# A batched matrix product: the first batch's x in two whole row tiles and a shared tile with a tail of eight small transfers

## The chip, the cores and the metric

The kernel runs on one core of a Trainium2 chip. The metric is the time of one execution on the device in microseconds (us); less is better. The core has five engines with their own instruction streams: PE (matrix products, with PEld for its weight loads), DVE, ACT, POOL and SP. Sixteen DMA engines move data between the chip's main memory (HBM) and the core's on-chip memory of 128 partitions; SP and POOL issue the transfers here, each on a queue of its own (q1 and q0 in the profile).

## The reference

`out[b] = x[b] @ weight[b]` for 32 batches, all in float32: x is 32 x 512 x 1024, weight is 32 x 1024 x 768, out is 32 x 512 x 768.

```python
def reference(x, weight):
    return np.matmul(x, weight).astype(np.float32)
```

In main memory that is 67.1 MB of x, 100.7 MB of weights and 50.3 MB of results, 218 MB in all, each read or written once.

## The kernel before

For each batch the 512 rows of x are divided into four row tiles of 128. Row `4*i + mt` belongs to tile `mt` and lies in partition `i`, so that a partition's four rows lie side by side in main memory (4 KB a row, 16 KB a partition). PE needs x with its long side (k) on the partitions, so each tile is first transposed on PE against an identity matrix (into PSUM, tile `pt`), and DVE copies the result to `xT` as bfloat16. Then 16 products for each row tile (8 steps of k, two shares of the 768 columns) go into PSUM banks (L123), and ACT and DVE copy the three banks of each pair of row tiles to `out_sb` (L143 to L145).

Weights come by POOL, cast to bfloat16 on the way, in one transfer of 3 MB (as read) for most batches (L70); four buffers. x comes by POOL in pairs of batches, 4 MB as read, also cast (L60); three buffers. Their transposes (L78) take two bfloat16 numbers as one 32-bit word. Results of two batches go out in one transfer by POOL (L164); those of the last four batches go out by SP (L182 to L185 and L216).

The order of the work is written out by hand (`manual_schedule`): each engine executes its instructions in the order of the program. POOL's first issues are w of batch 0, x of batches 1 and 2, w of 1 and 2, x of 3 and 4, w of 3, x of 5 and 6. The sixth and later ones wait for buffers: x of 5 and 6 for that of batch 0's first tiles, w of batch 4 for that of batch 0, which is free when PE has done batch 0, and so on. Batch `b`'s w is issued three batches ahead.

Batch 0 is the exception that the change concerns. Its x comes by SP, uncast, in float32, with transfers that carry no other batch: `x_first` (shown as `x_sb`, in the x pool) holds row tiles 0 to 2, 12 KB a partition, in one transfer (L151); `x_fourth` (shown as `one_sb`, in a pool with one buffer that is used again for the results of batch 30) holds row tile 3, 4 KB a partition, in 17 transfers (L154): 32, 16 and 16 partitions, twice two, and twelve times five, whose partitions are four apart. `transpose_first` takes a tile from one or the other (L101), does eight transposes (L105) and two casts (L106). PE transposes tiles 0 to 2 before its first product; tile 3 is transposed when its products are due:

```python
if b == 0:
    xT = {mt: transpose_first(mt) for mt in range(MT - 1)}
```

The kernel's lines that matter:

Of the kernel before, what the change touches and what calls it, by code (L numbers as in the profile page):

```python
# [8 lines left out]
F32 = mybir.dt.float32  # L9
# [4 lines left out]
def kernel(  # L14
# [6 lines left out]
    nc = tc.nc  # L21
    B, M, K = x.shape
    _, _, N = weight.shape
    P = 128
    MT = M // P
# [10 lines left out]
    x_pool = ctx.enter_context(tc.tile_pool(name="x", bufs=3))  # L36
    xT_pool = ctx.enter_context(tc.tile_pool(name="xT", bufs=6))
    out_pool = ctx.enter_context(tc.tile_pool(name="out", bufs=3))
    one_pool = ctx.enter_context(tc.tile_pool(name="one", bufs=1))
# [7 lines left out]
    x_view = x.rearrange("b (mi mo) k -> b mi mo k", mi=P)  # L47
# [6 lines left out]
    def banks():  # L54
        return [mpsum.tile([P, 512], F32, name=f"pm{i}") for i in range(3)]

    def load_pair(b):

        xs[b] = x_pool.tile([P, 2 * MT, K], BF16, name="x_sb")
        nc.gpsimd.dma_start(out=xs[b], in_=pair_view[b // 2])  # L60

    def load_last():
        xs[B - 1] = x_pool.tile([P, MT, K], BF16, name="x_sb")
        nc.gpsimd.dma_start(out=xs[B - 1], in_=x_view[B - 1])  # L64

    def load_w(b):
        ws[b] = w_pool.tile([P, KT, N], BF16, name="w_sb")
        at = 0
        for n in CHUNKED.get(b, (KT,)):
            nc.gpsimd.dma_start(out=ws[b][:, at:at + n, :], in_=w_view[b, :, at:at + n, :])  # L70
            at += n
# [9 lines left out]
    def transpose_pair(b, mt):  # L81

        both = xT_pool.tile([P, 2, JT, P // 2, 2, 2], BF16, name="xT")
        for half in range(2):
            nc.vector.tensor_copy(  # L85
                both[:, :, :, :, half, :].rearrange("p b j i r -> p j b i r"),
                words(b, mt + MT * half).rearrange("p j (b i r) -> p j b i r", b=2, r=2),
            )
        return [both[:, r].rearrange("p j i h r -> p j (i h) r") for r in range(2)]

    def transpose_last(mt):
        xT = xT_pool.tile([P, JT, P, 2], BF16, name="xT")
        nc.vector.tensor_copy(  # L93
            xT.rearrange("p j m r -> p (j m r)"), words(B - 1, mt).rearrange("p j m -> p (j m)")
        )
        return xT

    def transpose_first(mt):

        xT = xT_pool.tile([P, JT, P, 2], BF16, name="xT")  # L100
        rows = x_first[:, mt] if mt < MT - 1 else x_fourth[:, 0]  # L101
        for h in range(2):
            pt = tpsum.tile([P, JT, P], F32, name="pt")
            for i in range(JT):
                nc.tensor.transpose(pt[:, i, :], rows[:, JT * h + i::KT], ident)  # L105
            nc.vector.tensor_copy(  # L106
                xT[:, 2 * h:2 * h + 2].rearrange("p j m r -> p j r m"),
                pt.rearrange("p (j r) m -> p j r m", r=2),
            )
        return xT  # L110
# [8 lines left out]
    def matmuls(pm, half, xT, b, kos, together):  # L119
        for ko in kos:  # L120
            for i, (bank, at, off, size) in enumerate(SPLITS[half]):
                shares = half == 1 and i == 0
                nc.tensor.matmul(  # L123
                    pm[bank][:, at:at + size],
                    xT[:, ko // 2, :, ko % 2],
                    ws[b][:, ko, off:off + size],
                    start=(ko == 0 and not (together and shares)),
                    stop=(ko == KT - 1),
                    skip_group_check=together,
                )  # L130

    def open_out(b):

        if b == B - 2:
            outs[b] = one_pool.tile([P, MT * N], F32, name="one_sb")
            return
        if b % 2 == 0 or b == B - 1:
            twos[b // 2] = out_pool.tile([P, 2, MT * N], F32, name="out_sb")
        outs[b] = twos[b // 2][:, b % 2]

    def evacuate(b, pair, pm):
        o = outs[b][:, pair * N2:(pair + 1) * N2]
        nc.scalar.copy(o[:, 0:512], pm[0])  # L143
        nc.vector.tensor_copy(o[:, 512:1024], pm[1])  # L144
        nc.scalar.copy(o[:, 1024:N2], pm[2])  # L145

    with tc.manual_schedule():

        x_first = x_pool.tile([P, MT - 1, K], F32, name="x_sb")
        x_fourth = one_pool.tile([P, 1, K], F32, name="one_sb")  # L150
        nc.sync.dma_start(x_first, x_view[0, :, :MT - 1])  # L151
        few = [slice(at, first + 20, 4) for first in (0, 20, 40) for at in range(first, first + 4)]
        for rows in (slice(64, 96), slice(96, 112), slice(112, P), slice(60, 62), slice(62, 64), *few):
            nc.sync.dma_start(x_fourth[rows, 0], x_view[0, rows, MT - 1])  # L154
        load_w(0)
        ident = const.tile([P, P], F32)
        make_identity(nc, ident)
        load_pair(1)
        load_w(1)
        load_w(2)  # L160
        load_pair(3)

        def store(at):
            nc.gpsimd.dma_start(out=two_view[at], in_=twos[at])  # L164

        ready = {}
        for b in range(B):
            if b % 2 and b + AHEAD + 1 < B:
                if b + AHEAD + 1 == B - 1:
                    load_last()  # L170
                else:
                    load_pair(b + AHEAD + 1)
            if b % 2 and 2 < b < B - HELD - AHEAD:
                store((b - 3) // 2)
            if b + AHEAD < B:
                load_w(b + AHEAD)
            if b == B - LATE:
                store(b // 2 - 2)
                store(b // 2 - 1)
            if b == B - 1:  # L180
                halves = [slice(pair * N2, (pair + 1) * N2) for pair in range(2)]
                nc.sync.dma_start(out_view[b - 1, :, halves[0]], outs[b - 1][:, halves[0]])  # L182
                for late in range(B - LATE, B - 2):
                    nc.sync.dma_start(out_view[late], outs[late])
                nc.sync.dma_start(out_view[b - 1, :, halves[1]], outs[b - 1][:, halves[1]])  # L185
            open_out(b)
            if b == 0:
                xT = {mt: transpose_first(mt) for mt in range(MT - 1)}
            elif b == B - 1:
                xT = {mt: transpose_last(mt) for mt in range(MT)}  # L190
            else:
                if b % 2:
                    for mt in range(MT):
                        ready[b, mt], ready[b + 1, mt] = transpose_pair(b, mt)
                xT = {mt: ready.pop((b, mt)) for mt in range(MT)}
            if b not in CHUNKED:
                for pair in range(2):
                    pm = banks()
                    for half in range(2):
                        mt = 2 * pair + half  # L200
                        if mt not in xT:
                            xT[mt] = transpose_first(mt)
                        matmuls(pm, half, xT[mt], b, range(KT), False)
                    evacuate(b, pair, pm)
                continue
            pms = [banks() for _ in range(2)]
            at = 0
            for n in CHUNKED[b]:
                last = at + n == KT
                for mt in range(MT):  # L210
                    matmuls(pms[mt // 2], mt % 2, xT[mt], b, range(at, at + n), True)
                    if last and mt % 2 == 1:
                        pair = mt // 2
                        evacuate(b, pair, pms[pair])
                        if b == B - 1:
                            nc.sync.dma_start(out_view[b, :, halves[pair]], outs[b][:, halves[pair]])  # L216
                at += n
# [30 lines left out]
```

## Time and profile before

| | before |
|---|---|
| median of 3 runs | 514.45 us (514.42 to 514.56) |
| profiled execution | 514.44 us |
| its span, first to last instruction | 512.7 us |
| PE busy (matmuls) | 435.4 us, 85% |
| DVE, ACT, POOL busy | 130.0, 76.1 and 39.1 us |
| main memory, read and written | 167.77 MB and 50.33 MB, 425 GB/s over the span |
| granted TensorE clock, mean | 0.94 |

The profile is that of one execution. The span is what lies between its first and its last instruction; 1.7 us of the execution lie around it. In the rows of engines each digit is the busy share of one of 40 equal slices in tenths. A line of the time order has start, length, engine, line, operation, what it writes and reads, and in brackets how long the engine sat idle before it and what ended that. In the rows of DMA queues stand the packets, the megabytes and the time that their packets took as a share of all sixteen engines. A packet is one run of bytes on one DMA engine; the trace has its start, its length, its size and its queue, but not which of the sixteen engines it was. A transfer ends with a 4-byte packet on each DMA engine that took part: its completion write.

### The profile page before, as it was taken

How to read it: one execution, taken by the hardware profiler on the slowest of the kernel's cores; microseconds unless marked ns; L12 is line 12 of the kernel's file. 1: busy time of each engine (PE TensorE's matmuls, PEld its weight loads, DVE VectorE, ACT ScalarE, POOL GpSimd, SP SyncE). 2: the span in 40 equal slices, each digit the busy share in tenths (PEclk: the TensorE clock that was granted, in tenths of full speed). 3: DMA queues.
4: the chain of work that ended last, by engine and by line, in shares of the span. 5: the costliest groups of instructions: out<-in, count | busy, mean ns of one | idle time of the engine just before them, and what ended most of it. 6: DMA issues, size and time to landing. Idle time of an engine off the chain costs nothing.

```text
span 512.7 us, 5785 instructions
## 1 busy us (share of the span) xinstructions
PE 435.4 (85%) x2576; PEld 278.7 (54%) x2576; DVE 130.0 (25%) x196; ACT 76.1 (15%) x129; POOL 39.1 (8%) x73
## 2 busy tenths in 40 slices
PE   1806999999999996997989989798898989999991
PEld 1504666666666663654646546464464645666660
DVE  0202324141515141320413205041040410514121
ACT  1100121212121201111111111111101111120201
POOL 3000010101010101001010000101001000010000
PEclk9956999999999998997999989899798998999997
DMA  8999999999999999999999999999999999999998
GB/s 240 224 221 213 218 220 216 333 221 310 243 218 336 215 324 231 228 325 220 330 223 234 318 223 334 217 247 304 221 333 218 258 295 220 331 215 212 320 427 345
DMA packets 12712, 135.63 MB, mean 265 GB/s; under 512 B 1296, under 2 KB 1296, under 8 KB 3088
## 3 DMA queue, kind: packets, MB, share of 16 engines
q0 software_dynamic: 11440, 126.88, 96.6%
q1 hardware_dynamic: 1248, 8.39, 4.1%
q8 instruction: 20, 0.33, 0.2%
q14 instruction: 4, 0.03, 0.0%
HBM read 167.77 MB, written 50.33 MB: 425 GB/s over the span
## 4 chain that ended last, share of the span: by engine, by line
PE 46%; DMA 37%; issue 8%; DVE 5%; another core or an unknown queue 1%; POOL 1%; ACT 0%; SPq 0%; POOLq 0%
PE pm L123 40%; DMA w_sb<-in_weight_dram 28%; DMA one_sb<-in_x_dram 8%; PE pt L78 5%; DVE xT L85 4%; DVE out_sb L144 1%; POOL out_dram L164 0%; PE pt L105 0%; POOL w_sb L70 0%; POOL x_sb L60 0%; DVE one_sb L144 0%; DVE xT L93 0%; ACT out_sb L145 0%; SPq L151 0%
## 5 line engine op out<-in xcount | busy, mean ns | idle before, releaser
L123 PE MATMUL pm<-w_sb,xT 128*128 128x256 bf16 (+1 forms) x2048 | 353.7, 336 | 26.4 <-DMA w_sb<-in_weight_dram 26.2
L123 PEld LDWEIGHTS <-xT 128*128 128x128 bf16 x2048 | 205.3, 101 | 170.3 <-DMA w_sb<-in_weight_dram 29.3
L144 DVE COPY out_sb<-pm 128x512 f32<-128x512 f32 x62 | 42.9, 691 | 317.6 <-PE pm L123 317.6
L78 PE MATMUL pt<-ident,x_sb 128*128 128x128 f32 x496 | 79.8, 302 | 10.5 <-DVE xT L85 10.2
L78 PEld LDWEIGHTS pt<-ident,x_sb 128*128 128x128 f32 x496 | 69.3, 209 | 21.5 <-DVE xT L85 18.7
L85 DVE COPY xT<-pt 128x1024 bf16<-128x1024 bf16 x120 | 77.4, 687 | 11.0 <-PE pt L78 11.0
L143 ACT COPY out_sb<-pm 128x512 f32<-128x512 f32 x62 | 36.3, 585 | 271.7 <-PE pm L123 271.7
L145 ACT COPY out_sb<-pm 128x512 f32<-128x512 f32 x62 | 36.3, 585 | 145.7 <-PE pm L123 145.6
L70 POOL DMA_DIRECT2D w_sb<-in_weight_dram x37 | 20.1, 544 | 404.8 <-PE pm L123 397.6
L105 PE MATMUL pt<-ident,one_sb 128*128 128x128 f32 x8 | 1.9, 421 | 19.1 <-DMA one_sb<-in_x_dram 19.1
L106 DVE CAST xT<-pt 128x512 bf16<-128x512 f32 x8 | 5.8, 733 | 34.6 <-PE pt L105 34.1
L105 PE MATMUL pt<-ident,x_sb 128*128 128x128 f32 x24 | 5.3, 383 | 10.5 <-DMA x_sb<-in_x_dram 10.3
L105 PEld LDWEIGHTS pt<-ident,one_sb 128*128 128x128 f32 x8 | 1.6, 219 | 19.4 <-issue 19.4
L164 POOL DMA_DIRECT2D out_dram<-out_sb x14 | 10.1, 719 | 6.7 <-ACT out_sb L143 3.5
L105 PEld LDWEIGHTS pt<-ident,x_sb 128*128 128x128 f32 x24 | 4.1, 209 | 11.5 <-issue 10.3
L60 POOL DMA_DIRECT2D x_sb<-in_x_dram x15 | 8.1, 539 | 10.9 <-DMA w_sb<-in_weight_dram 10.9
L144 DVE COPY one_sb<-pm 128x512 f32<-128x512 f32 x2 | 1.4, 690 | 9.0 <-PE pm L123 9.0
L93 DVE COPY xT<-pt 128x1024 bf16<-128x1024 bf16 x4 | 2.6, 686 | 0.2 <-PE pt L78 0.2
L143 ACT COPY one_sb<-pm 128x512 f32<-128x512 f32 x2 | 1.2, 585 | 6.4 <-PE pm L123 6.4
L145 ACT COPY one_sb<-pm 128x512 f32<-128x512 f32 x2 | 1.2, 585 | 1.6 <-PE pm L123 1.6
L143 ACT ACT_TABLE_LOAD x1 | 1.3, 1283 | 0.7 <-PEq L232 0.7
L64 POOL DMA_DIRECT2D x_sb<-in_x_dram x1 | 0.5, 528 | 2.1 <-DMA w_sb<-in_weight_dram 2.1
(6 smaller groups left out, 0.9 us busy)
## 6 DMA issues: line engine op xcount, KB each, us to landing
w_sb<-in_weight_dram POOLq DMA_DIRECT2D x28, 1536.0 KB, 41.7
out_dram<-out_sb POOLq DMA_DIRECT2D x14, 3072.0 KB, 55.3
x_sb<-in_x_dram POOLq DMA_DIRECT2D x15, 2048.0 KB, 49.8
w_sb<-in_weight_dram POOLq DMA_DIRECT2D x7, 768.0 KB, 38.2
out_dram<-out_sb SPq DMA_DIRECT2D x2, 1536.0 KB
x_sb<-in_x_dram SPq DMA_DIRECT2D x1, 1536.0 KB
out_dram<-one_sb SPq DMA_DIRECT2D x2, 768.0 KB
out_dram<-out_sb SPq DMA_DIRECT2D x2, 768.0 KB
```

The source lines that it names most:

```text
L60: nc.gpsimd.dma_start(out=xs[b], in_=pair_view[b // 2])
L70: nc.gpsimd.dma_start(out=ws[b][:, at:at + n, :], in_=w_view[b, :, at:at + n, :])
L78: nc.tensor.transpose(pt[:, j, :], pairs[:, mo, j::JT], ident)
L85: nc.vector.tensor_copy(both[:, :, :, :, half, :].rearrange("p b j i r -> p j b i r"), words(b, mt + MT * half).rearrange("p j (b i r) -> ...
L93: nc.vector.tensor_copy(xT.rearrange("p j m r -> p (j m r)"), words(B - 1, mt).rearrange("p j m -> p (j m)"))
L105: nc.tensor.transpose(pt[:, i, :], rows[:, JT * h + i::KT], ident)
L106: nc.vector.tensor_copy(xT[:, 2 * h:2 * h + 2].rearrange("p j m r -> p j r m"), pt.rearrange("p (j r) m -> p j r m", r=2),)
L123: nc.tensor.matmul(pm[bank][:, at:at + size], xT[:, ko // 2, :, ko % 2], ws[b][:, ko, off:off + size], start=(ko == 0 and not (together an ...
L143: nc.scalar.copy(o[:, 0:512], pm[0])
L144: nc.vector.tensor_copy(o[:, 512:1024], pm[1])
L145: nc.scalar.copy(o[:, 1024:N2], pm[2])
L164: nc.gpsimd.dma_start(out=two_view[at], in_=twos[at])
```

## The change

`x_first` holds two row tiles instead of three, each brought by a transfer of its own: 128 rows of 4 KB. The other two tiles share the buffer of `one_sb`, now called `x_second`, with rows of 8 KB. It comes in 16 transfers instead of 17: five of 16 partitions (48 to 127), one of four, two of two, and eight of five partitions (0 to 39) instead of twelve. SP issues them in that order, after the two of `x_first`. PE transposes two tiles instead of three ahead of its first product; tiles 2 and 3 are transposed when their products are due. Nothing else differs.

```diff
     def transpose_first(mt):
...
-        rows = x_first[:, mt] if mt < MT - 1 else x_fourth[:, 0]
+        rows = x_first[:, mt] if mt < 2 else x_second[:, mt - 2]
...
-        x_first = x_pool.tile([P, MT - 1, K], F32, name="x_sb")
-        x_fourth = one_pool.tile([P, 1, K], F32, name="one_sb")
-        nc.sync.dma_start(x_first, x_view[0, :, :MT - 1])
-        few = [slice(at, first + 20, 4) for first in (0, 20, 40) for at in range(first, first + 4)]
-        for rows in (slice(64, 96), slice(96, 112), slice(112, P), slice(60, 62), slice(62, 64), *few):
-            nc.sync.dma_start(x_fourth[rows, 0], x_view[0, rows, MT - 1])
+        x_first = x_pool.tile([P, 2, K], F32, name="x_sb")
+        x_second = one_pool.tile([P, 2, K], F32, name="one_sb")
+        for mt in range(2):
+            nc.sync.dma_start(x_first[:, mt], x_view[0, :, mt])
+        many = [slice(at, at + 16) for at in range(48, P, 16)]
+        some = [slice(40, 44), slice(44, 46), slice(46, 48)]
+        few = [slice(at, first + 20, 4) for first in (0, 20) for at in range(first, first + 4)]
+        for rows in (*many, *some, *few):
+            nc.sync.dma_start(x_second[rows], x_view[0, rows, 2:])
...
-                xT = {mt: transpose_first(mt) for mt in range(MT - 1)}
+                xT = {mt: transpose_first(mt) for mt in range(2)}
```

## The prediction

> **What bounds the kernel now.** I read the page first, for the two rows that are full or nearly so:
>
> ```profile
> span 512.7 us, 5785 instructions
> PE 435.4 (85%) x2576; PEld 278.7 (54%) x2576; DVE 130.0 (25%) x196; ACT 76.1 (15%) x129; POOL 39.1 (8%) x73
> DMA  8999999999999999999999999999999999999998
> q0 software_dynamic: 11440, 126.88, 96.6%
> q1 hardware_dynamic: 1248, 8.39, 4.1%
> q8 instruction: 20, 0.33, 0.2%
> HBM read 167.77 MB, written 50.33 MB: 425 GB/s over the span
> ```
>
> PE is 85% busy. The sixteen DMA engines are full from the first slice to the last, and what they do is fixed by the program: POOL's queue (q0: weights, x, most stores), SP's queue (q1: first x, last stores) and twenty instruction fetches of 16 KB. So the end is when the last of the sixteen engines has done its own share.
>
> Second, the first 50 us, PE by order of time:
>
> ```profile
> 10.34 5.41 PE L105 MATMUL pt<-ident,x_sb 128*128 128x128 f32 x24 [10.34 <-DMA x_sb<-in_x_dram]
> 15.86 7.96 PE L123 MATMUL pm<-w_sb,xT 128*128 128x512 bf16 x48
> 42.90 1.94 PE L105 MATMUL pt<-ident,one_sb 128*128 128x128 f32 x8 [19.08 <-DMA one_sb<-in_x_dram]
> 44.81 4.41 PE L123 MATMUL pm<-w_sb,xT 128*128 128x256 bf16 x16
> ```
>
> PE waits 19 us for the fourth row tile. Looks like the thing to gain, but is not: third, POOL's issues by order of time.
>
> ```profile
> 49.52 0.53 POOL L70 DMA_DIRECT2D w_sb<-in_weight_dram  x1 [32.95 <-PE pm L123]
> 65.60 0.53 POOL L70 DMA_DIRECT2D w_sb<-in_weight_dram  x1 [15.55 <-PE pm L123]
> ```
>
> PE's lateness delays these issues (w of batches 4 and 5), but the trace's completion writes (packets of 4 B) show that what POOL issued earlier keeps the engines busy until about 65 and 73 us. The margin is 16 us at the first and 7 us at the second; no DMA engine misses PE there. The chain of waits has PE alone until 145 us and long DMA pieces for w after it: PE catches up, then follows the DMAs.
>
> Fourth, the end, by stretches of half a microsecond (the two columns before the last are PE's clock and the DMA share):
>
> ```profile
> 508.50:509.00 0.50, 0.00 (x0) 0.00 (x0) 0.00 (x0) 0.00 (x0) 0.00 (x0) 0.50 0.91 381
> 509.50:510.00 0.50, 0.00 (x0) 0.00 (x0) 0.00 (x0) 0.00 (x0) 0.00 (x0) 0.50 0.79 332
> 510.00:510.50 0.50, 0.00 (x0) 0.00 (x0) 0.00 (x0) 0.00 (x0) 0.00 (x0) 0.50 0.59 246
> 510.50:511.00 0.50, 0.00 (x0) 0.00 (x0) 0.00 (x0) 0.00 (x0) 0.00 (x0) 0.50 0.35 147
> 511.00:511.50 0.50, 0.00 (x0) 0.00 (x0) 0.00 (x0) 0.00 (x0) 0.00 (x0) 0.50 0.06 25
> ```
>
> The engines stop one after the other: their last completion writes are at 508.7 (two), 509.1, 510.1 to 510.5 (seven), 511.0 to 511.4 (six). A change that shifts bytes between engines moves the end by what the last engine gets, not by the mean.
>
> **Who is last, and why.** The small transfers of five rows run on five engines. Transfer by transfer (queues in 28.5 to 30.4 us):
>
> ```profile
> q1 hardware_dynamic: 10, 0.02, 3.2%
> ```
>
> Five packets of 4 KB and five completion writes, in 1.98 us: each waits its turn behind one weight packet (0.91 us), both times. [...] So call engines 0 to 4 the low ones. After the small transfers they lag: the sixteen completion writes of batch 3's w fall in 55.6 to 56.2 us (ten), 56.8 (one) and 57.8 to 58.1 (five), some 1.9 to 2.1 us behind. The others catch that lag up later: each instruction fetch (0.2% of 16 x 512.7 us over 20 is about 0.8 us, 0.9 in the packets) sets one engine back by about 1.1 us. Following the sorted completion writes from one transfer to the next, the steps fall on eight engines in turn, two or three times each, never on the low five or on three others, which are the early ones at the end. By this reading the last six are mostly fetchers with three steps, and one or two low engines 0.05 to 0.4 us ahead of the very last.
>
> **The change, part by part.** Costs by packet in the trace: 12 KB 0.460 us, 4 KB 0.172 us, less 0.019 overlap with the packet before: 0.441 and 0.153. 8 KB from SP into SBUF is not seen; on the line between them it is 0.297. (Bounds: 0.294, two thirds of the 12 KB packet, and 0.306, two 4 KB packets; I take the line.) A completion write 0.01.
>
> Removed, per engine: x_first's 8 packets of 12 KB (8 x 0.441 = 3.53); the fourth tile's 18 packets on engines 0 and 1 (2.75), 16 on 2 to 4 (2.45), 4 on the others (0.61). With completions 6.48, 6.16 and 4.18; the model's lag of the low ones is 2.30 and 1.98, measured about 2.1 and 1.9, so it is good to some 10%.
> Added: 16 packets of 4 KB on all (2.45); 8 KB packets: 16 on engines 0 and 1 (5 + 1 + 2 + 8), 14 on 2 and 3, 13 on 4, 5 on the rest, that is 4.75, 4.16, 3.86, 1.49. With completions 7.40, 6.79, 6.48, 4.02.
> Difference: +0.92 on engines 0 and 1, +0.63 on 2 and 3, +0.32 on 4, -0.16 on the other eleven; +0.09 in the mean.
>
> Bytes are the same; the tail of small transfers shifts 8 to 24 KB more to the low engines. At the end, a low engine that was 0.3 us ahead of the last becomes 0.92 - 0.3 = 0.6 us later than the old end. Sum: +0.6 us on the span, 513.3.
>
> **Moved, at no cost.** SP issues 18 transfers where it issued 18 (2 + 16 for 1 + 17); SP has nothing else before 486.86 us. PE: 24 + 8 transposes become 16 + 16, the same 32. x_first lands earlier: until 6.0 us only SP's queue runs, and 64 KB an engine at 0.153 per 4 KB from 1.8 us with 0.5 us of first latency end near 5 us, where 96 KB ended at 9.8. PE then does the two tiles' transposes by about 9, but waits for w of batch 0 until 15 anyway. x_sb's slot comes free by 10 instead of 15.8, so POOL issues its x (16.04 now) earlier, behind a full queue: nothing. x_second: from 6 us on, engine 0 has some 27 turns left instead of 38; at the 33 POOL packets seen in those 38 (0.91 each for w, 1.21 for x), 23 to 24 of them plus 4.6 us of its own give about 34.5 us instead of 42.4. Then PE has two tiles to do instead of one: 6.15 us as now (42.90 to 49.05), plus 1.8 for transposes, 0.8 for a cast (733 ns) and 2.65 for 16 matmuls (7.96 x 16/48): the batch ends near 46.4 instead of 49.05. PE is 2.7 us earlier; the queue it feeds was 7 us ahead, so the gain goes nowhere. If this cover went, each us of a late x_second beyond about 40 + 5 would cost a us. Stores: the last ones are issued at 501.16 to 502.8 and their engines come free for them from 506.4; a w that lands 0.6 us later on one engine is still 3 us early.
>
> Profiled execution: 514.44 us, 1.74 around the span; the median of the runs is 514.45, so the forecast is 515.05 us. A tell-apart bound of 0.2% is 1.03 us here: 513.42 to 515.48.
>
> **Rivals.**
> (a) The fetchers stay last: the low engines' lag has shrunk by the end by more than I read (some extra steps of 0.3 to 0.6 us, on the low engines too, belong to 8 KB fetches whose engine could differ). Then the end moves by -0.16 to +0.1: 514.3 to 514.55. For it: the very last engine has the pattern of a fetcher. Against: six engines end within 0.45 us.
> (b) Slower: the low engines 0 and 1 are themselves last already, or take a fetch more. Then the whole 0.92 counts, with 8 KB at 0.306 it is 1.07, and 16 turns that start at the same first latency as 8 do up to 0.3 more: 515.4 to 515.9. It decides where the low ones end less than 0.1 us ahead of the others now. The lag measured (2.45 for the worst two, with three fetches 3.3 behind the other side) speaks against, not strongly.
> (c) Slower by starvation: 4 KB packets at the start run at the 0.3 to 0.5 us seen for first packets rather than 0.153; 2 us of a half-filled start on every engine, +1 to 2 us: 515.5 to 516.5. The DMA share of 0.56 in 2 to 3 us shows that the start isn't full even with 12 KB; the full rate from 4 us on is against. x_second after 45 us would add to this, from that point 1 for 1.
> (d) It doesn't do what it says: 8 KB rows go out as two packets of 4 KB. Then 16 data turns become 32, x_second lands near 34.5 + 16 x 0.8 = 47, the batch ends near 59, w of batch 5 is issued near 76 with the queue empty at 73: 3 us lost, 518. 12 KB rows went as one packet, so unlikely.
> (e) Faster by over 0.2%: would need 1 us less on the last engine; nothing in the sum has it. An earlier PE is no gain while the DMA row is full.
>
> **How the numbers follow.** Chances: main case 0.42, (a) 0.20, (b) 0.19, (c) 0.13, (d) 0.03, (e) 0.03. The range that leaves out 2 in 10 runs from the low end of (a) into (c): 514.2 to 516.1; the main case alone 514.75 to 515.5. Slower by over 0.2% (above 515.48) is most of (b) and (c), (d), and a little of the main case: 0.33; faster 0.04; same 0.63.
>
> **What would show it.** Right: x_sb's wait on PE near 5 us, one_sb's near 35, the last L123 of batch 0 near 46; the DMA row as full as now; POOL's w issues after 200 us at the same times or up to 1 us later; completion writes with five engines 2.5 to 3 us behind after 40 us; and the DMA share in the last us falling to one or two engines (0.06 to 0.12) for over half a us. Wrong: a dip of the DMA row before 80 us (c, d), a DMA share in 2 to 5 us far below 0.56 to 1.00, or last completion writes in the old order with the old spread (a).

## The result and the profile after

The change makes the kernel slower: 517.79 us (517.51 to 517.87) against 514.50 us (514.42 to 514.57), a ratio of 1.0063 with a 95% interval of 1.0046 to 1.0080. That is 3.3 us more, and above the forecast range of 514.2 to 516.1. The profiled execution took 517.75 us, its span is 516.0 us.

The page of the changed kernel, the rows that answer to those shown of before:

```profile
span 516.0 us, 5786 instructions
PE 436.1 (85%) x2576; PEld 279.0 (54%) x2576; DVE 129.8 (25%) x196; ACT 76.3 (15%) x129; POOL 39.2 (8%) x73
DMA  9999999999999999999999999999999999999997
q0 software_dynamic: 11440, 126.88, 96.4%
q1 hardware_dynamic: 1408, 8.39, 4.8%
HBM read 167.77 MB, written 50.33 MB: 423 GB/s over the span
```

Bytes and work are the same and the DMA row is just as full. So the DMA engines were busy for longer over the same bytes. Both queues show it: q1's packets took 24.8 us of each engine's time (4.8% of 516.0) instead of 21.0 (4.1% of 512.7), with 160 packets more; q0's took 497.4 us instead of 495.3, with the same 11440 packets.

PE by order of time in the first 54 us, and POOL's next issues:

```profile
5.20 3.53 PE L105 MATMUL pt<-ident,x_sb 128*128 128x128 f32 x16 [5.20 <-DMA x_sb<-in_x_dram]
19.10 6.71 PE L123 MATMUL pm<-w_sb,xT 128*128 128x512 bf16 x32 [10.37 <-DMA w_sb<-in_weight_dram]
43.15 1.95 PE L105 MATMUL pt<-ident,one_sb 128*128 128x128 f32 x8 [17.34 <-DMA one_sb<-in_x_dram]
51.12 2.78 PE L123 MATMUL pm<-w_sb,xT 128*128 128x256 bf16 x16 [0.38 <-DVE xT L106]
```

```profile
54.20 0.53 POOL L70 DMA_DIRECT2D w_sb<-in_weight_dram  x1 [44.63 <-PE pm L123]
70.26 0.53 POOL L70 DMA_DIRECT2D w_sb<-in_weight_dram  x1 [15.53 <-PE pm L123]
```

x_first is there at 5.2 us as forecast, but the weights of batch 0, waited for until 15 us by the forecast, let PE start only at 19.10 us, and x_second, there at 42.7 us instead of 34.5, lets PE go on at 43.15. Batch 0 ends at 53.7 us. POOL's issue at 70.26 us is still ahead of its queue (w of batch 4 begins to be complete at 75.4 us by the completion writes), so PE does not starve the DMA engines; something in the first 20 us does. The stretches of both kernels show it (the last two columns are the DMA share and GB/s as seen in on-chip memory; a share above 1 means that packets overlap in time on one engine). Before:

```profile
6.00:10.00 4.00, 0.00 (x0) 0.00 (x0) 0.00 (x0) 0.00 (x0) 0.00 (x0) 1.00 1.09 259
10.00:15.00 5.00, 4.57 (x20) 3.54 (x20) 2.96 (x5) 0.00 (x0) 0.00 (x0) 1.00 1.09 248
15.00:20.00 5.00, 4.85 (x30) 3.08 (x31) 1.41 (x2) 0.58 (x1) 0.53 (x1) 1.00 1.02 221
```

After:

```profile
6.00:10.00 4.00, 2.73 (x14) 2.05 (x13) 2.79 (x4) 0.00 (x0) 0.54 (x1) 1.00 1.29 201
10.00:15.00 5.00, 0.00 (x0) 0.00 (x0) 0.00 (x0) 0.00 (x0) 0.00 (x0) 0.66 1.33 198
15.00:20.00 5.00, 0.90 (x3) 0.40 (x3) 0.00 (x0) 0.00 (x0) 0.00 (x0) 0.50 1.13 177
```

The engines are busier by the clock (1.29 and 1.33) and move a fifth less. This is the time of x_second's five transfers of 16 partitions. From the trace's single packets that start in 6 to 18 us:

| | before | after |
|---|---|---|
| x_fourth or x_second from SP, packet size | 4 KB | 8 KB |
| its packets, median and longest | 0.172, 0.172 us | 0.646, 1.096 us |
| weight packets, median and longest | 0.925, 1.086 us | 1.182, 1.548 us |
| weight packets over 1 us | 7 of 125 | 89 of 112 |
| completion writes from SP, longest | 0.022 us | 1.374 us |

When x's last small transfers run alone among five engines, from 22 us on, its 8 KB packets take 0.322 us and the weights' 0.926 us again. The loss is made in 6 to 20 us and nearly all of it is kept to the end: all sixteen completion writes of w of batch 2 are later than before, by 3.3 us in the mean (42.88 against 39.62 us), and the last completion writes of the sixteen engines by 3.2 us (513.65 against 510.48). The end by stretches has before's shape, moved:

```profile
513.00:513.50 0.50, 0.00 (x0) 0.00 (x0) 0.00 (x0) 0.00 (x0) 0.00 (x0) 0.50 0.68 283
513.50:514.00 0.50, 0.00 (x0) 0.00 (x0) 0.00 (x0) 0.00 (x0) 0.00 (x0) 0.50 0.38 160
514.00:514.50 0.50, 0.00 (x0) 0.00 (x0) 0.00 (x0) 0.00 (x0) 0.00 (x0) 0.50 0.18 74
```

### The profile page after: what moved, and what is told of

Same layout as the page of the kernel before. It is cut to its first block, busy times and chain, and to the rows that moved or that the text cites. A ratio compares the mean times of both kernels' runs of the same rounds, so it can differ in the third digit from the quotient of the medians.

```text
span 516.0 us, 5786 instructions
## 1 busy us (share of the span) xinstructions
PE 436.1 (85%) x2576; PEld 279.0 (54%) x2576; DVE 129.8 (25%) x196; ACT 76.3 (15%) x129; POOL 39.2 (8%) x73
## 3 DMA queue, kind: packets, MB, share of 16 engines
q0 software_dynamic: 11440, 126.88, 96.4%
## 4 chain that ended last, share of the span: by engine, by line
PE 56%; DMA 27%; DVE 6%; issue 5%; another core or an unknown queue 3%; POOL 1%; ACT 0%; SPq 0%; POOLq 0%
PE pm L123 50%; DMA w_sb<-in_weight_dram 18%; DMA one_sb<-in_x_dram 7%; PE pt L78 6%; DVE xT L85 4%; DVE out_sb L144 1%; DMA x_sb<-in_x_dram 1%; PE pt L105 0%; POOL out_dram L167 0%; POOL x_sb L60 0%; POOL w_sb L70 0%; DVE xT L106 0%; DVE one_sb L144 0%; DVE xT L93 0%
## 5 line engine op out<-in xcount | busy, mean ns | idle before, releaser
L78 PE MATMUL pt<-ident,x_sb 128*128 128x128 f32 x496 | 79.8, 303 | 10.4 <-DVE xT L85 10.1
L78 PEld LDWEIGHTS pt<-ident,x_sb 128*128 128x128 f32 x496 | 69.3, 209 | 21.5 <-DVE xT L85 18.7
L105 PE MATMUL pt<-ident,one_sb 128*128 128x128 f32 x16 | 3.0, 350 | 17.3 <-DMA one_sb<-in_x_dram 17.3
L105 PE MATMUL pt<-ident,x_sb 128*128 128x128 f32 x16 | 3.5, 396 | 5.2 <-DMA x_sb<-in_x_dram 5.2
L105 PEld LDWEIGHTS pt<-ident,x_sb 128*128 128x128 f32 x16 | 2.9, 212 | 5.7 <-issue 5.2
```

Of the source, the lines that this page charges most:

```text
L78: nc.tensor.transpose(pt[:, j, :], pairs[:, mo, j::JT], ident)
```

## The experiments

The theory after the result (A): each of the five transfers has all sixteen engines write into 16 adjacent partitions at once (80 packets of 8 KB between 6 and 18 us; the first transfer's sixteen completion writes start at 7.26 to 8.72 us), and such writes hold each other up. Rivals: (B) the reading side, 8 KB pieces 16 KB apart; (C) 8 KB packets as such; (D) the two transfers of `x_first`.

**Writing side or reading side.** Three kernels, each from the changed one: both sides spread over every fifth partition, the writing side alone, the reading side alone. In the last two some rows of batch 0 land in each other's places, so batch 0's results come out in another order; bytes and packets are the same.

```diff
-        many = [slice(at, at + 16) for at in range(48, P, 16)]
+        many = [slice(at, P, 5) for at in range(48, 53)]
```

```diff
+        for i in range(5):
+            nc.sync.dma_start(x_second[48 + i:P:5], x_view[0, many[i], 2:])   # writing side
... or, in the third kernel
+            nc.sync.dma_start(x_second[many[i]], x_view[0, 48 + i:P:5, 2:])   # reading side
...
-        for rows in (*many, *some, *few):
+        for rows in (*some, *few):
```

> The changed kernel, but each of the five transfers of 16 partitions takes every fifth partition from 48 on instead of 16 adjacent ones; same bytes, same engines, same order. Theory A (sixteen engines write into 16 adjacent partitions at once[...]): the long packets between 6 and 20 us go back to 0.33 us (8 KB) and 0.93 us (w), w of batch 0 lands near 15 us, time about 515.0 (514.7 to 515.5). Theory B (they read 8 KB pieces that lie 16 KB apart in main memory): gaps become 80 KB, so it could go either way, 515 to 517.8. Theory C (8 KB packets cost this wherever they go) and D (the two transfers of x_first, 4 KB packets, cost it): 517.8.

> Only the writing side is spread: source rows adjacent as in the changed kernel, destinations every fifth partition (80 partitions of two row tiles of batch 0 hold each other's rows, so batch 0's results are of permuted rows). A: 515.0, as with both sides spread. B, C, D: 517.8.

> Only the reading side is spread: destinations 16 adjacent partitions as in the changed kernel, source rows every fifth (batch 0's rows permuted). A: 517.8, packets as long as in the changed kernel. B: 515.0. C, D: 517.8.

Measured: both spread 514.84 us (514.63 to 515.09), ratio to before 1.0005 (0.9996 to 1.0013); writing side alone 514.84 us, 1.0003 (0.9995 to 1.0012); reading side alone 517.47 us, 1.0057 (1.0042 to 1.0072). Both spread, by stretches; below it the writing side alone; last the reading side alone:

```profile
6.00:10.00 4.00, 3.07 (x14) 2.29 (x13) 2.92 (x4) 0.00 (x0) 0.54 (x1) 1.00 1.07 256
10.00:15.00 5.00, 0.00 (x0) 0.00 (x0) 0.00 (x0) 0.00 (x0) 0.00 (x0) 1.00 1.03 254
15.00:20.00 5.00, 4.86 (x16) 2.24 (x16) 0.00 (x0) 0.00 (x0) 0.00 (x0) 1.00 1.03 226
```

```profile
8.00:10.00 2.00, 0.73 (x5) 0.56 (x5) 1.33 (x2) 0.00 (x0) 0.54 (x1) 1.00 1.07 256
10.00:15.00 5.00, 0.00 (x0) 0.00 (x0) 0.00 (x0) 0.00 (x0) 0.00 (x0) 0.67 1.03 254
15.00:20.00 5.00, 4.87 (x20) 2.46 (x20) 0.00 (x0) 0.51 (x1) 0.00 (x0) 0.64 1.03 226
```

```profile
6.00:10.00 4.00, 3.13 (x14) 2.35 (x13) 2.92 (x4) 0.00 (x0) 0.54 (x1) 1.00 1.24 207
10.00:15.00 5.00, 0.00 (x0) 0.00 (x0) 0.00 (x0) 0.00 (x0) 0.00 (x0) 1.00 1.31 205
15.00:20.00 5.00, 1.76 (x6) 0.80 (x6) 0.00 (x0) 0.00 (x0) 0.00 (x0) 1.00 1.15 197
```

With the writes spread none of these packets is long: 8 KB at most 0.322 us, weights at most 0.925 us in 6 to 18 us, the same with the writing side alone. With the reads spread and the writes adjacent, 82 of 112 weight packets stay over 1 us. PE of the kernel with both sides spread starts its products four microseconds earlier than in the changed kernel, and its next transposes 3.5:

```profile
15.14 7.72 PE L123 MATMUL pm<-w_sb,xT 128*128 128x512 bf16 x32 [6.07 <-DMA w_sb<-in_weight_dram]
39.66 1.94 PE L105 MATMUL pt<-ident,one_sb 128*128 128x128 f32 x8 [16.79 <-DMA one_sb<-in_x_dram]
```

The place of the writes accounts for 2.95 us of the 3.3; C falls, and so does B as the cause (spreading the reads alone gave 0.3 us, with overlapping runs, and nothing once the writes are spread).

**The other new part.** `x_first` in one transfer again, alone and together with the spread.

```diff
-        for mt in range(2):
-            nc.sync.dma_start(x_first[:, mt], x_view[0, :, mt])
+        nc.sync.dma_start(x_first, x_view[0, :, :2])
```

> The changed kernel with x_first's two tiles in one transfer (8 KB rows) instead of two; the rest unchanged. D: about 515. A, B, C: 517.4 to 518.0; by the packet prices 16 x 0.153 = 2.45 us become 8 x 0.297 = 2.38, so at most 0.1 us less.

> Both undone: x_first in one transfer and the five transfers spread. If the 0.86 us that one transfer for x_first gave came from the crowded time alone (other phases of the engines against each other): 514.7 to 514.9, as the spread kernel. Rival, one transfer is worth that by itself: 513.9 to 514.1.

Measured: alone 516.93 us (516.63 to 517.33), ratio 1.0046 (1.0031 to 1.0061), so 0.86 us less than the changed kernel where 0.1 at most was expected. With the spread it is 515.18 us (514.86 to 515.73), ratio 1.0012 (1.0005 to 1.0019): no gain over the spread kernel, rather 0.3 us more (more on these below, under the low engines). So one transfer is worth nothing by itself. It makes the crowded time cheaper: only 13 of its 118 weight packets are over 1 us, though its 8 KB packets are still at 0.508 us. Why one form crowds less (other phases of the engines against each other, as the expectation had it) was not taken further.

**Dose: half the spread, and smaller packets.** Four of the five transfers over every second partition; and the adjacent transfers cut in two, with 4 KB packets.

```diff
-        many = [slice(at, at + 16) for at in range(48, P, 16)]
+        many = [slice(at, at + 32, 2) for at in (48, 49, 80, 81)] + [slice(112, P)]
```

> A dose: four of the five transfers of 16 take every second partition (16 spread over 32), the fifth stays 16 adjacent ones (112 to 127). Theory A[...] only the fifth transfer costs, a fifth of the 2.95 us between the changed kernel and the fully spread one: 515.3 to 515.5. Rival, cost in proportion[...]: half of four fifths and a fifth, 516.6. Rival, only the full spread helps: 517.5 or more.

```diff
+        for mt in range(2):
+            for rows in many:
+                nc.sync.dma_start(x_second[rows, mt], x_view[0, rows, 2 + mt])
-        for rows in (*many, *some, *few):
+        for rows in (*some, *few):
```

> The changed kernel with each of the five transfers of 16 adjacent partitions cut into two, one for each row tile, so that 16 adjacent partitions are still written at once but with 4 KB packets; the rest stays at 8 KB. Theory A[...] 4 KB packets stay at 0.17 us and w at 0.93, no loss before 20 us, as seen with the 4 KB packets of the kernel before. Rival, adjacency alone lengthens packets whatever their size. Either way ten more turns (five data, five completions) of about 0.9 us bring x_second at some 48 us (39 in the spread kernel), batch 0 ends near 58, the w of batch 5 is issued near 75 when the queue has run dry at 72.5, so the queue stands still for 3 to 5 us: 517.8 to 520 in all. A dip in the DMA row between 70 and 85 us shows that share, and the packet lengths the other.

Measured: half the spread 515.05 us (514.96 to 515.33), ratio 1.0009 (1.0003 to 1.0016), less than the 515.3 to 515.5 expected. The stretches show the four spread transfers at full rate, and the loss only where the fifth falls:

```profile
6.00:10.00 4.00, 3.10 (x14) 2.31 (x13) 2.93 (x4) 0.00 (x0) 0.53 (x1) 1.00 1.07 256
10.00:15.00 5.00, 0.00 (x0) 0.00 (x0) 0.00 (x0) 0.00 (x0) 0.00 (x0) 1.00 1.09 236
15.00:20.00 5.00, 3.68 (x13) 1.72 (x13) 0.00 (x0) 0.00 (x0) 0.00 (x0) 1.00 1.03 197
```

At w of batch 2 the completion writes are 0.83 us later in the mean than in the fully spread kernel, where five adjacent transfers make them 3.43 us later: one costs a quarter of five, near the fifth that was expected. At the end 0.37 us of it are left, and 0.21 in time, mostly because the fully spread kernel loses 0.38 us in a later place where this one does not (below, under the low engines).

With 4 KB packets into the same adjacent partitions the x packets have a median of 0.172 us and no weight packet in 6 to 18 us is over 0.925. So adjacency alone is not enough. The time is 522.71 us all the same (522.24 to 523.62), ratio 1.0158 (1.0141 to 1.0174), more than the 517.8 to 520 expected. The stretches show why:

```profile
65.00:70.00 5.00, 5.00 (x34) 3.35 (x33) 1.50 (x3) 0.58 (x1) 0.00 (x0) 1.00 1.01 215
70.00:75.00 5.00, 5.00 (x33) 2.99 (x31) 0.69 (x1) 1.17 (x2) 0.00 (x0) 1.00 0.63 133
75.00:80.00 5.00, 5.00 (x33) 3.04 (x32) 0.69 (x1) 1.17 (x2) 1.76 (x3) 1.00 0.47 75
80.00:85.00 5.00, 5.00 (x32) 2.97 (x31) 0.69 (x1) 1.17 (x2) 0.00 (x0) 1.00 0.98 209
```

x_second is complete at 49.2 us, POOL's w for batch 5 is issued at 76.71 us, and the queue had run dry at 73.6 us in the mean of the engines:

```profile
76.71 0.53 POOL L70 DMA_DIRECT2D w_sb<-in_weight_dram  x1 [15.54 <-PE pm L123]
```

The engines stand still for 0.37 x 5 + 0.53 x 5 = 4.5 us. Against the spread kernel, w of batch 5 lands 5.3 us later and the engines end 7.0 us later in the mean. The trace has most of the rest in longer packets of POOL's own queue: weight packets between 75 and 80 us add 0.58 us for each engine, packets of 16 KB from 80 us on 1.83 us, against 0.48 in the spread kernel (all beyond the usual 0.926 and 1.227 us). Why these are long is not shown.

What the runs show is that 16 adjacent partitions crowd at 8 KB (x packets 0.646 us in the median, 201 GB/s in 6 to 10 us), and that 16 of 32 (256 GB/s there, as with the full spread) and 4 KB (0.172 us) do not. Why adjacent partitions crowd was not shown: no run measured the rate at which a group of partitions takes writes, or tried other groupings.

**Is the kernel before touched by this?** Its transfers of 32, 16 and 16 adjacent partitions, spread.

```diff
-        for rows in (slice(64, 96), slice(96, 112), slice(112, P), slice(60, 62), slice(62, 64), *few):
+        for rows in (slice(64, P, 2), slice(65, P, 4), slice(67, P, 4), slice(60, 62), slice(62, 64), *few):
```

> The kernel before, its transfers of 32, 16 and 16 adjacent partitions taking every second, fourth and fourth partition from 64 on. Its 4 KB packets show no lengthening (0.172 us throughout), so by theory A nothing changes: 514.4 to 514.6. Rival, adjacency costs at 4 KB too: 513.5 to 514.2.

Measured 514.60 us (514.48 to 514.78), ratio 1.0001 (0.9992 to 1.0009). It isn't.

**Which engines end last.** The spread kernel is 0.3 us above before (not told apart from it by its interval). In its trace the four last engines are low ones by my following of the completion writes. So I took packets from them.

```diff
-        many = [slice(at, P, 5) for at in range(48, 53)]
-        some = [slice(40, 44), slice(44, 46), slice(46, 48)]
-        few = [slice(at, first + 20, 4) for first in (0, 20) for at in range(first, first + 4)]
+        many = [slice(at, P, 6) for at in range(32, 38)]
+        some = [slice(at, 32, 3) for at in range(20, 23)]
+        few = [slice(at, first + 20, 4) for first in (0,) for at in range(first, first + 4)]
```

> The spread kernel with less on the low engines: six transfers of 16 (every sixth partition from 32 on), three of four, four of five; so 8 KB packets 13 on engines 0 to 3, 10 on engine 4, 6 on the others, instead of 16, 14, 13 and 5. If in the spread kernel the low engines end last, as the prediction said of the changed kernel, by about 0.9 us in its trace: 514.1 (513.9 to 514.4), as fast as the kernel before or a little faster. Rival, the engines with instruction fetches end last: one packet more on them, 515.0 to 515.2.

Measured 514.83 us (514.68 to 515.06), ratio 1.0006 (0.9997 to 1.0015): no gain. The lag of the low engines did fall: the spread of the sixteen completion writes of batch 2's w went from 3.6 us to 2.4 us. But two engines, by the same following one low engine and one with fetches, now end 0.5 us behind all others (511.69 and 511.76 us; the next is 511.19), and the mean is 510.54 us. Neither theory of the expectation gave this; which engine is last stays open. No kernel tried here is faster than the one before.

## Why the prediction was wrong

**What bounds the kernel** was read rightly: the DMA engines do. PE's wait for x_second was worth nothing as a place to gain, and the queue never ran dry in the changed kernel. So the two early signs of being wrong that were named, a dip of the DMA row before 80 us and a low share in 2 to 5 us (it was 0.76 to 0.99), did not appear; the engines were full and slow. The run with 4 KB pieces showed the cover's edge: x_second at 49.2 us, 4 us beyond the 45 that the prediction named, cost 4.5 us of still engines and 7 in the end.

**The step that failed** is the price of the five transfers of 16 partitions: "8 KB from SP into SBUF is not seen; on the line between them it is 0.297", used as five packets on each engine at 1.49 us, with bounds of 0.294 and 0.306. Alone, or spread, the packet takes 0.322 us less the overlap of 0.019, 0.303: the line was good. In its place it took 0.646 in the median, the completion writes priced at 0.01 took up to 1.374, and what had not been priced at all, the weight packets beside it, took 1.182 instead of 0.925. Over the run, for each engine, the 8 KB packets took 3.87 us instead of the spread kernel's 2.56, SP's completion writes 2.91 instead of 0.24, and POOL's 12 KB packets 1.8 us more; these overlap, so they come to more than the loss. The bounds were bounds on a packet, where the cost was that of sixteen packets into 16 adjacent partitions at once. The prediction counted which engines move the bytes and never asked which partitions they write. It gave the eleven other engines -0.16 us; the mean over all sixteen was +3.2 us, of which the place of the writes is 2.95 in time.

**The low engines' share** was forecast as +0.6 us at the end and +0.09 in the mean (its terms as printed add up to 0.10). With the writes spread, the last completion write is 0.43 us later than before (511.84 against 511.41) and the mean 0.20 (510.68 against 510.48). In time it is 0.3 us, within the interval of no change. The size is of the forecast order, but the trace does not show the forecast's reason for it. It shows on how many engines a transfer ran (SP's 224 completion writes before and 256 after are those of 16, 5, 4 and 2 a transfer, by its rows) and not on which: that the small ones all fall on the same few, numbered from 0, was the author's assumption (the lag of five engines agrees), and the packets and microseconds for engines 0 to 4 are estimates that rest on it. At w of batch 2 the engines of the spread kernel are 0.17 us earlier in the mean than before. They lose 0.38 us between 87 and 92 us, where SP moves nothing: packets of 16 KB there (x of batches 7 and 8, from POOL) take up to 1.914 us instead of 1.227, and in the kernel before none there is longer than 1.227. The kernel with x_first in one transfer and the spread loses 0.71 us in that place, 0.33 more, about as much as it is slower; the one with less on the low engines loses 0.32 there, so taking packets from these left that loss as it was. Why the packets were long there is open.

**x_second at 34.5 us** failed by two terms. "Some 27 turns left" at 6 us took it that two or three 8 KB packets would be through by then; the completion writes of x_first's second tile come at 5.1 to 5.9 us and the first 8 KB packet at 6.0, so all 32 turns were left. That is 39.2 us in the spread kernel. The other 3.5 us to 42.7 are the crowded time. It cost nothing at the end, as the working said.

**The rivals.** (c) named a slow start with 4 KB packets and a cost of 1 to 2 us; neither came: the packets of x_first took 0.159 us in the median from 4 to 6 us, and the loss was 3.3 us. (d) has the figure nearest to the measured one, 518, but that is chance: 8 KB went as one packet (128 packets of 8 KB for x_second's 128 rows) and no queue ran dry. The 4 KB pieces, with ten turns more where (d) has sixteen, took 522.71 us, so 518 was too low for that case. (a) and (b) concern fractions of a us, which the missed term covers up. That a transfer's destination could be the bound had no rival.

## What to carry to other kernels

Where all sixteen DMA engines are full, look at which partitions a small transfer writes at the same moment, not only at its bytes, packet size and number of engines: five transfers to 16 adjacent partitions at 8 KB cost 2.95 us for 0.66 MB here, every fifth partition lengthened no packet of theirs, nor did 4 KB rows, and the edit is one slice. The price taken from the line between two packet sizes held here (0.303 against 0.297) only alone or where the writes were spread; crowded, the packet took 0.646 in the median. And in 10 to 15 us the DMA share was higher than before (1.33 against 1.09) while the GB/s were lower (198 against 248): the same 12 KB weight packets took 1.182 us in the median from 6 to 18 us and 0.926 from 22 us on. Where a stretch looks like that, compare its packets with the same ones elsewhere in the trace before explaining the end.

## What the runs showed that was not expected

The crowded writes lengthened other packets than their own. The weights go to all 128 partitions, of which each of the five transfers writes an eighth. But 89 of the 112 weight packets in that time were over 1 us (112 are seven for each engine if shared evenly, so at least thirteen engines had long ones), and 4-byte completion writes took up to 1.374 us instead of 0.022. How the one holds up the other was not shown: the trace tells neither which engine a packet ran on nor where it wrote.

Packets were long without any small transfer beside them too. The 16 KB packets between 87 and 92 us (up to 1.914 us in the spread kernel against 1.227 before), alone in POOL's queue, cost 0.31 to 0.71 us for each engine in the four kernels that wrote x_second's 8 KB rows fully spread and nothing in the kernel before, the changed one and the one with half the spread. The differences of a few tenths of a us between these kernels are of that size; whether the spread brings the long packets about is open.
